# A two-layer decoder trunk on one core: which engine splits the first weights of a stage, and where GpSimd's work stands at the mixers' ends

## The chip, the cores and the metric

The kernel runs on one core of a Trainium2 chip. The core has a matrix engine (TensorE, PE in the profile), three engines for elementwise work (VectorE or DVE, ScalarE or ACT, GpSimd or POOL) and a queue that issues transfers (SyncE or SP). Each runs its own list of instructions in order and waits for others at semaphores. The metric is device time in microseconds; the median of three runs before the change is 2029.25 us.

## The reference, cut to what matters

Two layers on x of 512 tokens by 1024 features, in float32. Each layer is feed-forward, token mixer, feed-forward, and each of these stands between two RMS norms:

```
hf = swiglu(rms_norm(x, g[0]), gate, up, down);  x = x + 0.5 * rms_norm(hf, g[1])
xn = rms_norm(x, g[2]);  mix = attention(xn) or mlstm(xn);  x = x + rms_norm(mix, g[3])
hf = swiglu(rms_norm(x, g[4]), gate, up, down);  x = x + 0.5 * rms_norm(hf, g[5])
swiglu(x) = (silu(x @ gate) * (x @ up)) @ down          # inner width 2816 = 22 x 128
```

Layer 0 mixes with attention (eight stick-breaking heads, eight dilated heads), layer 1 with an mLSTM. So there are six stages, called f00, att, f01, f10, mls and f11 in the code.

## The kernel before, in words

Every float32 factor of a product is split in two: a high part, rounded by a cast on ScalarE (whi, xnh, hhi, dhi), and the rest, found by a subtraction (wlo, xnl, hlo, dlo). A product is then three TensorE instructions: high by high, high by low, low by high (`mm3`). A weight chunk of 128 by 1024 is loaded by SP into one of three buffers called raw, cast to whi on ScalarE, and subtracted to wlo (`chunk`). A raw buffer is free for the next load when the subtraction is done, and a whi buffer (four of them inside a stage) when TensorE has used it.

The tokens are in four blocks of 128 (tb 0 to 3). x and the stage's result y are kept with tokens on partitions; xnh and xnl hold the normalized x transposed. TensorE transposes it into PSUM (tiles pt), ScalarE copies the high part and VectorE takes the low part from PSUM. The first products of a stage go over its first weights twice, for tokens 0 to 255 (the first half) and for 256 to 511.

Between two stages stands, for each block, a chain: y gets its last product (po, added by VectorE from PSUM), y times the gain is yg, ScalarE sums the squares, GpSimd takes the inverse root r of a 128x1 column, VectorE updates x; then squares, root and gain again give the input of the transposition. Behind a feed-forward this is `chain` and `pre` (L276 writes xa and xb, L281 transposes), and the first four chunks of the next stage come from `first_chunks`, with the subtraction on GpSimd, pinned in program order. The first of mls is a small gate chunk, always on VectorE. Behind a mixer it is `out_last`, written out by hand: `load`, `hi` and `lo` are the three steps of a chunk (six chunks, numbered 0 to 5), `add`, `sq`, `mul`, `root`, `upd` and `xs` the chain's, `tp` the transposition (L614), `xn` the two parts of xnh and xnl. Operations on VectorE, ScalarE and GpSimd in there are pinned in the written order and have the line number L51 of the helper that pins them.

The order of everything else is set by a planner that walks a clock of TensorE time and wakes waiting tasks; the table W holds delays for it. `l2` and `l3` say how long after the written part the transpositions of blocks 2 and 3 come in TensorE's list.

Of the kernel before, what the change touches and what calls it, by code (L numbers as in the profile page):

```python
# [24 lines left out]
OFF, OFFV = 80, 48  # L25
# [7 lines left out]
STARTE = (0, 3)  # L33
# [4 lines left out]
       "g6", "o2", "g7")  # L38
W = dict(pdf=9000, pda=4000, pdm=4000, lane=14464, sb1=11880, sb2=6132, d1=14281, d2=3450, qs=6662, end=2121, tz=12960, m0=7140, m1=9600, m2=4263,
         cv=12909, og=1942, mend=5400, avs=2127, mvs=3369, ac1=4899, mc1=4987, ac2=3992, mc2=4402, fc1=5500, fc2=4500,  # L40
         pre=3900, l2=12800, l3=15800, x00=6863, x01=5227, x02=1924, x03=0, x10=7176, x11=2670, x12=1796, x13=0)


class Pinned:
# [9 lines left out]
class Trunk:  # L54
# [109 lines left out]
    def first_chunks(self, ph, between=None, pool=None):  # L164

        a, g = self.a, self.nc.gpsimd
        if ph == "att":
            srcs = [(a["attn_in"][c], 1024) for i in ORD[:2] for c in ((i, 4 + i) if i < 4 else (8 + i, 12 + i))]
        elif ph == "mls":
            srcs = [(a["gates"], 0)] + [(a["mlstm_in"][i], 1024) for i in (0, 8, 1)]  # L170
        else:
            l, w = int(ph[1]), int(ph[2])
            srcs = [(a[n][l, w, f], 1024) for f in (0, 1) for n in ("gate", "up")]
        self.cs = []

        def task():
            for i, (s, n) in enumerate(srcs):
                self.cs.append(self.chunk(s, pool=pool, shift=OFF, eng=None if between and i in STARTE else g) if n else
                               self.gates(s))
                if between and i:  # L180
                    between(i + 1) if i < 3 else None
                yield W["x%s%d" % (ph[1], i)] if pool else self.w_pre
        self.spawn(task(), 0 if pool or between else W["pd" + ph[0]])
        self.tick()
# [23 lines left out]
    def gain(self, l, i, pool=None):  # L208
        wide = pool and pool is self.xpool
        g = (pool or self.pp).tile([P, D], F32, tag="gb" if wide else "dr" if pool else "gp", bufs=1,  # L210
                                   name="gb")
        self.nc.sync.dma_start(g, self.a["norm_g"][l * 6 + i:l * 6 + i + 1, :].partition_broadcast(P))
        return g
# [75 lines left out]
    def half(self, h):  # L289

        self.require(lambda: {2 * h, 2 * h + 1} <= self.xn_done)
        if h:
            self.xn_done.clear()
# [252 lines left out]
    def out_last(self, ws, mix, po, done, nxt, gain):  # L546
# [5 lines left out]
        g = gain(None)  # L552
        xp = self.xpool = tc.alloc_tile_pool(name="xp", bufs=1, side="right", reuse_waits="tile")
        V, A, G = [Pinned(tc, e) for e in (nc.vector, nc.scalar, nc.gpsimd)]
# [4 lines left out]
        def load(i):  # L559
            raws[i] = self.pp.tile([P, 1024], F32, tag="raw", bufs=3, name="raw")  # L560
            nc.sync.dma_start(raws[i], srcs[i])

        def hi(i):
            pool = xp if i < 4 else None
            self.cs.append([self.whole(t, t, OFF - 64 if pool else OFF, pool) for t in ("whi", "wlo")])
            A.copy(self.cs[i][0], raws[i])

        def lo(i, e):
            e.tensor_sub(self.cs[i][1], raws[i], self.cs[i][0])
# [4 lines left out]
        def add(tb, h):  # L574
            V.tensor_add(self.y[:, tb, half(h)], self.y[:, tb, half(h)], po[tb][h])

        def square(src, h, ss):
            junk = self.pp.tile([P, 512], mybir.dt.bfloat16, tag="junk", bufs=1, name="junk")
            A.activation(junk, src[:, half(h)], AF.Square, accum_out=ss)

        def sq(tb, h, x=False):
            if x:
                ss = self.sums[:, tb, h:h + 1]
            else:
                ss = vs[tb, h] = self.few(self.pp, 1, "ss", 4)
            square((self.x if x else self.y)[:, tb, :], h, ss)

        def mul(tb, h, e):
            if h == 0:
                ygs[tb] = [xp.tile([P, 512], F32, tag="h", bufs=4, name="yg") for _ in range(2)]  # L590
            e.tensor_mul(ygs[tb][h], self.y[:, tb, half(h)], g[:, half(h)])

        def root(tb, x=False):
            acc = EPS
            for h in range(2):
                v = self.few(self.pp, 1, "v", 4)
                V.tensor_scalar(v, self.sums[:, tb, h:h + 1] if x else vs[tb, h], 1.0 / D, acc,
                                op0=ALU.mult, op1=ALU.add)
                acc = v
            rs[tb] = self.few(self.pp, 1, "r", 4)  # L600
            G.tensor_tensor(rs[tb], v, self.mhalf, op=ALU.pow)

        def upd(tb, h):
            xt = self.x[:, tb, half(h)]
            V.scalar_tensor_tensor(xt, ygs[tb][h], rs[tb], xt, op0=ALU.mult, op1=ALU.add)

        def xs(tb, h):
            V.scalar_tensor_tensor(ygs[tb][h], self.x[:, tb, half(h)], rs[tb], gn[:, half(h)],
                                   op0=ALU.mult, op1=ALU.mult)

        def tp(tb, h):
            pts[tb, h] = pt = self.bank("pt")
            for j in range(4):
                nc.tensor.transpose(pt[:, j * P:(j + 1) * P], ygs[tb][h][:, j * P:(j + 1) * P], self.ident)  # L614
                self.clk += 109

        def xn(tb, h, part):
            dst = [c[:, 4 * h:4 * h + 4, tb * P:(tb + 1) * P] for c in (self.xnh, self.xnl)]
            src = pts[tb, h].rearrange("p (k t) -> p k t", k=4)
            if part:  # L620
                V.tensor_sub(dst[1], src, dst[0])
            else:
                A.copy(dst[0], src)
# [5 lines left out]
            self.out_part(ws, mix, po, tb, ks)  # L629
        hi(0)  # L630
        lo(0, G)
        hi(1)
        load(2)
        load(3)
        add(0, 0); sq(0, 0); add(0, 1); sq(0, 1)
# [2 lines left out]
        mul(0, 1, V)  # L638
        root(0)
        add(1, 1); sq(1, 1)  # L640
        mul(1, 0, G)
        upd(0, 0); sq(0, 0, True); upd(0, 1); sq(0, 1, True)
        mul(1, 1, V)
        root(1)
# [4 lines left out]
        tp(0, 0); tp(0, 1)  # L649
        xn(0, 0, 0); xn(0, 1, 0)  # L650
        xs(1, 0); xs(1, 1)
        tp(1, 0); tp(1, 1)
        xn(0, 0, 1); xn(0, 1, 1)
        xn(1, 0, 0); xn(1, 1, 0)
        hi(2)
        lo(1, G)
        hi(3)
        xn(1, 0, 1); xn(1, 1, 1)
        self.xn_done |= {0, 1}

        load(4)
        lo(3, G)
        add(2, 0); sq(2, 0); add(2, 1); sq(2, 1)
        add(3, 0); sq(3, 0); add(3, 1); sq(3, 1)
        lo(2, V)
        load(5)
        mul(2, 0, G); mul(3, 0, G)
        mul(2, 1, V); mul(3, 1, V)
        root(2)
        hi(4)  # L670
        upd(2, 0); sq(2, 0, True); upd(2, 1); sq(2, 1, True)
        root(3)
        lo(4, V)
        upd(3, 0); sq(3, 0, True); upd(3, 1); sq(3, 1, True)
        hi(5)
        root(2, True)
        root(3, True)
        xs(2, 0); xs(2, 1)
        lo(5, V)
        xs(3, 0); xs(3, 1)  # L680

        def late(tb, wait):
# [615 lines left out]
```

## Time and profile before

| what | value |
|---|---|
| runs | 2024.54, 2029.25, 2032.24 us |
| profiled execution | 2027.32 us, of which the span of the trace is 2025.6 us |
| TensorE busy | 1965.8 us, 97% |
| VectorE, ScalarE, GpSimd busy | 1318.1, 954.5, 498.2 us |
| mean granted clock of TensorE | 0.99 of full speed |

TensorE has work nearly all the time, so the time that can be won by moving other engines' work lies in the few places where it waits or runs at half clock. These are the ends of stages. The engines of a row say who worked; in the timeline, the bracket behind a row gives the idle time of the engine before it, and what ended that.

### The profile page before, as it was taken

The page shows a single profiled execution, that of the slowest core. Times are in us where ns is not written, and L with a number is a line of the kernel's source. Part 1 is how long each engine was busy: PE and PEld are TensorE (multiplying, and loading weights), DVE is VectorE, ACT ScalarE, POOL GpSimd, SP SyncE. Part 2 cuts the span into 40 slices and gives each one's busy share as a digit, 9 for nine tenths or more (in the row PEclk, how much of TensorE's full clock was granted, in tenths as well). Part 3 has the DMA queues.
Part 4 walks back from the last instruction along what each step waited for, and adds up shares of the span by engine and source line. Part 5 has one row for each costly group of instructions (what it writes and reads, how often), then busy time and mean ns, then how long its engine had stood idle before and what let it go on. Part 6 is the DMA issues. An engine that isn't in the chain of part 4 may idle for free. (4 is left out here: it accounts for less than half of the span.)

```text
span 2025.6 us, 25972 instructions
## 1 busy us (share of the span) xinstructions
PE 1965.8 (97%) x9876; PEld 1664.9 (82%) x9876; DVE 1318.1 (65%) x2018; ACT 954.5 (47%) x1649; POOL 498.2 (25%) x372
## 2 busy tenths in 40 slices
PE   8999999999999999999999999999999999999998
PEld 7888888888887878888788888888889878888887
DVE  6766654666678775664487666547776787676643
ACT  5443333477786453333244333324887644433321
POOL 4332312101002342221343232121010143332111
PEclk9999999999999999999999999999999999999999
DMA  5423332232221333233123333321423222433321
GB/s 180 132 94 105 104 111 75 81 113 68 68 73 58 108 122 108 96 110 117 54 84 126 104 104 105 115 68 54 154 100 126 92 85 96 132 94 114 105 84 42
DMA packets 56119, 200.51 MB, mean 99 GB/s; under 512 B 6521, under 2 KB 6649, under 8 KB 55994
## 3 DMA queue, kind: packets, MB, share of 16 engines
q1 hardware_dynamic: 55992, 198.85, 29.8%
q8 instruction: 77, 1.26, 0.3%
q14 instruction: 48, 0.39, 0.1%
q10 hardware_dynamic: 2, 0.00, 0.0%
HBM read 196.65 MB, written 4.80 MB: 99 GB/s over the span
## 5 line engine op out<-in xcount | busy, mean ns | idle before, releaser
L83 PE MATMUL pg<-xnh,whi 128*128 128x512 f32 (+1 forms) x1568 | 576.8, 369 | 3.9 <-ACT xnh L51 2.0
L83 PE MATMUL pg<-xnh,wlo 128*128 128x512 f32 (+1 forms) x1568 | 577.1, 368 | 3.4 <-DVE wlo L51 3.4
L83 PE MATMUL pg<-xnl,whi 128*128 128x512 f32 (+1 forms) x1568 | 577.5, 369 | 0.9 <-DVE xnl L205 0.5
L148 ACT CAST whi<-raw 128x1024 fp32r<-128x1024 f32 x236 | 247.5, 1051 | 430.6 <-issue 190.7
L149 DVE TENSOR_TENSOR wlo<-raw,whi 128x1024 fp32r<-128x1024 f32 x223 | 284.9, 1279 | 185.9 <-ACT whi L148 181.8
L83 PEld LDWEIGHTS pg<-xnh,wlo 128*128 128x128 f32 x1568 | 297.0, 189 | 53.5 <-DVE wlo L51 4.2
L83 PEld LDWEIGHTS pg<-xnh,whi 128*128 128x128 f32 x1568 | 296.4, 190 | 54.1 <-ACT xnh L51 2.9
L83 PEld LDWEIGHTS pg<-xnl,whi 128*128 128x128 f32 x1568 | 297.3, 190 | 50.3 <-DVE xnl L51 1.0
L414 POOL TENSOR_TENSOR h<-h,rs 128x512 f32<-128x512 f32 x88 | 143.1, 1626 | 755.7 <-ACT h L413 755.7
L205 DVE TENSOR_TENSOR dlo<-raw,dhi 128x512 fp32r<-128x512 f32 x240 | 189.4, 809 | 88.9 <-ACT dhi L204 88.5
L204 ACT CAST dhi<-raw 128x512 fp32r<-128x512 f32 x240 | 146.6, 622 | 195.8 <-DMA raw<-down 152.1
L415 DVE TENSOR_TENSOR h<-h,pg 128x512 f32<-128x512 f32 x88 | 60.0, 682 | 205.7 <-PE pg L83 197.2
L83 PE MATMUL pc<-dhi,hhi 128*128 128x512 f32 x448 | 175.2, 391 | 5.1 <-ACT hhi L204 5.1
L83 PE MATMUL pc<-dhi,hlo 128*128 128x512 f32 x448 | 175.1, 391 | 0.3 <-DVE hlo L205 0.3
L83 PE MATMUL pc<-dlo,hhi 128*128 128x512 f32 x448 | 174.9, 390 | 0.0
L499 DVE TENSOR_TENSOR y<-y,pc 128x512 f32<-128x512 f32 x192 | 128.6, 677 | 5.5 <-PE pc L83 5.4
L83 PE MATMUL pq<-xnh,whi 128*128 128x512 f32 (+1 forms) x312 | 109.9, 353 | 0.8 <-DVE ql L791 0.8
L83 PE MATMUL pq<-xnl,whi 128*128 128x512 f32 (+1 forms) x312 | 109.7, 352 | 0.3 <-DVE xnl L205 0.3
L83 PE MATMUL pq<-xnh,wlo 128*128 128x512 f32 (+1 forms) x312 | 109.2, 350 | 0.0
L205 DVE TENSOR_TENSOR hlo<-h,hhi 128x256 fp32r<-128x256 f32 x208 | 103.1, 514 | 8.1 <-ACT hhi L204 7.9
L204 ACT CAST hhi<-h 128x256 fp32r<-128x256 f32 x208 | 78.9, 404 | 55.2 <-DVE h L415 48.3
L83 PEld LDWEIGHTS pc<-dhi,hhi 128*128 128x128 f32 x448 | 84.4, 188 | 23.3 <-ACT hhi L204 6.0
(257 smaller groups left out, 3318.4 us busy)
## 6 DMA issues: line engine op xcount, KB each, us to landing
raw<-gate SPq DMA_DIRECT2D x88, 512.0 KB, 3.4
raw<-up SPq DMA_DIRECT2D x88, 512.0 KB, 3.4
raw<-down SPq DMA_DIRECT2D x88, 512.0 KB, 3.5
raw<-mlstm_in SPq DMA_DIRECT2D x24, 512.0 KB, 3.5
raw<-attn_in SPq DMA_DIRECT2D x16, 512.0 KB, 3.4
bt<-rows SPq DMA_DIRECT2D x8, 896.0 KB, 4.2
gb<-norm_g SPq DMA_DIRECT2D x11, 512.0 KB, 3.6
raw<-attn_v SPq DMA_DIRECT2D x8, 512.0 KB, 9.0
```

Source lines behind the costliest of these rows:

```text
L83: self.nc.tensor.matmul(out, lhsT=lhsT, rhs=rhs, start=start, stop=stop, skip_group_check=True)
L148: nc.scalar.copy(hi[:, :n], raw[:, :n])
L149: sub = (eng or nc.vector).tensor_sub(lo[:, :n], raw[:, :n], hi[:, :n])
L204: self.nc.scalar.copy(hi, src)
L205: self.nc.vector.tensor_sub(lo, src, hi)
L414: self.nc.gpsimd.tensor_mul(h, h, self.rs)
L415: self.nc.vector.tensor_mul(h, h, pu)
L499: self.nc.vector.tensor_add(dst, dst, b)
```

## The change

Three things change. Behind a feed-forward, the first chunks of the next stage are subtracted on VectorE, where the planner may place them, and no longer on GpSimd. At a mixer's end, GpSimd gives three of its four products of y with the gain to VectorE and keeps the roots and three subtractions (chunks 0, 1 and 2; before 0, 1 and 3), and the casts and subtractions stand at other places. And block 2's transposition is planned later (`l2`, `l3`).

```
-  pre=3900, l2=12800, l3=15800, ...
+  pre=3900, l2=15000, l3=16500, ...
 first_chunks:
-  self.chunk(s, pool=pool, shift=OFF, eng=None if between and i in STARTE else g) if n else ...
+  self.chunk(s, pool=pool, shift=OFF, eng=g if between and i not in STARTE else None) if n else ...
 out_last:
         hi(0)
         lo(0, G)
-        hi(1)
...
-        mul(1, 0, G)
+        mul(1, 0, V)
...
         xs(1, 0); xs(1, 1)
+        hi(1)
+        lo(1, G)
         tp(1, 0); tp(1, 1)
...
         hi(2)
-        lo(1, G)
-        hi(3)
+        lo(2, G)
...
+        add(2, 0); sq(2, 0); add(2, 1); sq(2, 1)
+        hi(3)
+        add(3, 0); sq(3, 0); add(3, 1); sq(3, 1)
         load(4)
-        lo(3, G)
...
-        lo(2, V)
         load(5)
-        mul(2, 0, G); mul(3, 0, G)
-        mul(2, 1, V); mul(3, 1, V)
+        lo(3, V)
         root(2)
+        mul(2, 0, V); mul(2, 1, V)
         hi(4)
         upd(2, 0); sq(2, 0, True); upd(2, 1); sq(2, 1, True)
         root(3)
         lo(4, V)
+        mul(3, 0, V); mul(3, 1, V)
+        hi(5)
         upd(3, 0); sq(3, 0, True); upd(3, 1); sq(3, 1, True)
-        hi(5)
         root(2, True)
+        lo(5, V)
         root(3, True)
         xs(2, 0); xs(2, 1)
-        lo(5, V)
         xs(3, 0); xs(3, 1)
```

On VectorE the four subtractions (wlo) now stand in the list of the old stage, beside the last gated products h and their splits hlo; this is the end of f00, and f01 reads alike.

```order
 L205 TENSOR_TENSOR hlo<-h,hhi 128x256 x2
 L205 TENSOR_TENSOR dlo<-raw,dhi 128x512 x2
-L415 TENSOR_TENSOR h<-h,pg 128x512
+L149 TENSOR_TENSOR wlo<-raw,whi 128x1024
+L415 TENSOR_TENSOR h<-h,pg 128x512
+L149 TENSOR_TENSOR wlo<-raw,whi 128x1024
 L205 TENSOR_TENSOR hlo<-h,hhi 128x256 x2
-L415 TENSOR_TENSOR h<-h,pg 128x512
+L149 TENSOR_TENSOR wlo<-raw,whi 128x1024
+L415 TENSOR_TENSOR h<-h,pg 128x512
```

So the subtractions have left the stretch of the chains and stand before the last split of h.

GpSimd's list at a mixer's end, before:

```order
L51 TENSOR_TENSOR wlo<-raw,whi 128x1024
L51 TENSOR_TENSOR yg<-y,gb 128x512
L51 TENSOR_TENSOR r<-v,mhalf 128x1
L51 TENSOR_TENSOR yg<-y,gb 128x512
L51 TENSOR_TENSOR r<-v,mhalf 128x1 x3
L51 TENSOR_TENSOR wlo<-raw,whi 128x1024 x2
L51 TENSOR_TENSOR yg<-y,gb 128x512 x2
L51 TENSOR_TENSOR r<-v,mhalf 128x1 x4
```

and after, up to the first product of the feed-forward:

```order
L51 TENSOR_TENSOR wlo<-raw,whi 128x1024
L51 TENSOR_TENSOR yg<-y,gb 128x512
L51 TENSOR_TENSOR r<-v,mhalf 128x1 x4
L51 TENSOR_TENSOR wlo<-raw,whi 128x1024 x2
L51 TENSOR_TENSOR r<-v,mhalf 128x1 x4
L414 TENSOR_TENSOR h<-h,rs 128x512 x2
```

Three products with the gain are gone, one between the first two roots and two before the last four.

ScalarE's list at the end of att, before, from the cast of chunk 4 (raw_5890) on; raw_6431 and raw_6462 are chunks 6 and 7, which the feed-forward itself loads:

```order
L51 CAST whi_5926<-raw_5890 128x1024
L51 ACTIVATE junk_5930,sums_75<-x_71 128x512
L51 ACTIVATE junk_5933,sums_75<-x_71 128x512
L51 ACTIVATE junk_5943,sums_75<-x_71 128x512
L51 ACTIVATE junk_5946,sums_75<-x_71 128x512
L51 CAST whi_5948<-raw_5910 128x1024
L51 CAST xnh_73<-pt_6102 128x4x128
L51 CAST xnh_73<-pt_6107 128x4x128
L148 CAST whi_6433<-raw_6431 128x1024
L51 CAST xnh_73<-pt_6137 128x4x128
L51 CAST xnh_73<-pt_6142 128x4x128
```

and after, where chunk 4 is raw_5907:

```order
L51 CAST whi_5922<-raw_5907 128x1024
L51 ACTIVATE junk_5926,sums_75<-x_71 128x512
L51 ACTIVATE junk_5929,sums_75<-x_71 128x512
L51 CAST whi_5942<-raw_5909 128x1024
L51 ACTIVATE junk_5946,sums_75<-x_71 128x512
L51 ACTIVATE junk_5949,sums_75<-x_71 128x512
L148 CAST whi_6433<-raw_6431 128x1024
L51 CAST xnh_73<-pt_6123 128x4x128
L51 CAST xnh_73<-pt_6128 128x4x128
L51 CAST xnh_73<-pt_6137 128x4x128
L51 CAST xnh_73<-pt_6142 128x4x128
```

The cast of chunk 6 stood between the copies of block 2 and block 3 and now stands before all four.

## Rows read from the trace of the kernel before

**Rows 1.** Windows: length, busy time (instructions) of PE, PEld, DVE, ACT, POOL, then clock.
```profile
640.00:680.00 40.00, 31.76 (x217) 28.80 (x216) 33.42 (x59) 17.78 (x37) 14.29 (x11) 0.91 0.27 90
685.00:690.00 5.00, 5.00 (x46) 5.00 (x46) 1.82 (x4) 1.42 (x3) 1.72 (x2) 1.00 0.47 189
975.00:1000.00 25.00, 25.00 (x112) 20.67 (x112) 9.94 (x14) 6.63 (x15) 7.45 (x6) 1.00 0.07 22
1000.00:1040.00 40.00, 35.23 (x214) 30.79 (x213) 32.53 (x54) 12.92 (x33) 15.60 (x14) 0.91 0.20 66
1014.00:1021.00 7.00, 5.91 (x19) 4.61 (x18) 5.27 (x10) 1.99 (x6) 1.83 (x2) 0.51 0.23 75
```

**Rows 2.** Waits of PE, f00 to att (335 to 372): total, times, longest.
```profile
PE pt L281 <- DVE xb L276: 1.2, 1, 1.2
PE po L83 <- ACT hhi L204: 1.1, 1, 1.1
PE pt L281 <- DVE xa L276: 0.6, 2, 0.4
```

**Rows 3.** Waits of PE, f01 to f10 (985 to 1030).
```profile
PE pt L281 <- DVE xa L276: 2.5, 1, 2.5
PE pt L281 <- DVE xb L276: 1.8, 2, 1.1
```

**Rows 4.** Timeline of DVE and POOL, end of f01: start, length, what.
```profile
992.78 2.40 POOL L149 TENSOR_TENSOR wlo<-raw,whi 128x1024 fp32r<-128x1024 f32 x1
992.85 3.54 DVE L306 SCALAR_TENSOR_TENSOR x<-yg,r,x 128x512 f32<-128x512 f32 x2 [0.66 <-POOL r L239]
...
1028.85 1.41 DVE L306 SCALAR_TENSOR_TENSOR x<-yg,r,x 128x512 f32<-128x512 f32 x2 [0.73 <-POOL r L239]
```

**Rows 5.** Timeline of DVE and POOL, end of att, blocks 0 and 1.
```profile
633.79 2.41 POOL L51 TENSOR_TENSOR wlo<-raw,whi 128x1024 fp32r<-128x1024 f32 x1 [48.10 <-PE po L83]
634.06 1.88 DVE L51 TENSOR_TENSOR y<-y,po 128x512 f32<-128x512 f32 x3 [0.59 <-PE po L83]
...
638.39 1.29 POOL L51 TENSOR_TENSOR yg<-y,gb 128x512 f32<-128x512 f32 x1
638.46 2.43 DVE L51 SCALAR_TENSOR_TENSOR x<-yg,r,x 128x512 f32<-128x512 f32 x2 [0.72 <-POOL r L51]
...
646.26 2.34 POOL L51 TENSOR_TENSOR wlo<-raw,whi 128x1024 fp32r<-128x1024 f32 x1
646.33 3.48 DVE L51 SCALAR_TENSOR_TENSOR yg<-x,r,gb 128x512 f32<-128x512 f32 x2 [0.66 <-POOL r L51]
```

**Rows 6.** Timeline of PE, ends of att and (from 1649) of mls.
```profile
644.67 1.32 PE L614 MATMUL pt<-ident,yg 128*128 128x128 f32 x8 [0.64 <-DVE yg L51]
649.20 1.97 PE L614 MATMUL pt<-ident,yg 128*128 128x128 f32 x8 [3.21 <-DVE yg L51]
...
651.72 0.58 PE L83 MATMUL pg<-xnl,whi 128*128 128x256 f32 x1
...
678.01 0.39 PE L83 MATMUL pg<-xnl,whi 128*128 128x256 f32 x1 [0.40 <-DVE xnl L51]
...
1649.91 1.31 PE L614 MATMUL pt<-ident,yg 128*128 128x128 f32 x8 [0.42 <-DVE yg L51]
...
1682.69 0.31 PE L83 MATMUL pg<-xnl,whi 128*128 128x256 f32 x1
```

**Rows 7.** Timeline, end of att: a root, and chunk 6.
```profile
663.47 1.22 DVE L51 TENSOR_TENSOR wlo<-raw,whi 128x1024 fp32r<-128x1024 f32 x1
663.70 1.39 POOL L51 TENSOR_TENSOR r<-v,mhalf 128x1 f32<-128x1 f32 x1 [1.98 <-DVE v L51]
...
670.23 0.33 SPq L146 DMA_DIRECT2D raw<-gate  x1
...
675.06 1.04 ACT L148 CAST whi<-raw 128x1024 fp32r<-128x1024 f32 x1 [2.86 <-DMA raw<-gate]
```

**Rows 8.** Page, part 6: issues, size, median us to landing.
```profile
raw<-gate SPq DMA_DIRECT2D x88, 512.0 KB, 3.4
```

More of the change, by code (lines that the diff above doesn't have):

```diff
@@ L40 @@
          cv=12909, og=1942, mend=5400, avs=2127, mvs=3369, ac1=4899, mc1=4987, ac2=3992, mc2=4402, fc1=5500, fc2=4500,
-         pre=3900, l2=12800, l3=15800, x00=6863, x01=5227, x02=1924, x03=0, x10=7176, x11=2670, x12=1796, x13=0)
+         pre=3900, l2=15000, l3=16500, x00=6863, x01=5227, x02=1924, x03=0, x10=7176, x11=2670, x12=1796, x13=0)
 class Pinned:
@@ L177, in task @@
             for i, (s, n) in enumerate(srcs):
-                self.cs.append(self.chunk(s, pool=pool, shift=OFF, eng=None if between and i in STARTE else g) if n else
-                               self.gates(s))
+                self.cs.append(self.chunk(s, pool=pool, shift=OFF, eng=g if between and i not in STARTE else None)
+                               if n else self.gates(s))
                 if between and i:
@@ L655, in out_last @@
         hi(2)
-        lo(1, G)
-        hi(3)
+        lo(2, G)
         xn(1, 0, 1); xn(1, 1, 1)
         self.xn_done |= {0, 1}
+        add(2, 0); sq(2, 0); add(2, 1); sq(2, 1)
+        hi(3)
+        add(3, 0); sq(3, 0); add(3, 1); sq(3, 1)
         load(4)
-        lo(3, G)
-        add(2, 0); sq(2, 0); add(2, 1); sq(2, 1)
-        add(3, 0); sq(3, 0); add(3, 1); sq(3, 1)
-        lo(2, V)
         load(5)
-        mul(2, 0, G); mul(3, 0, G)
-        mul(2, 1, V); mul(3, 1, V)
+        lo(3, V)
         root(2)
+        mul(2, 0, V); mul(2, 1, V)
         hi(4)
```

## The prediction

> **What bounds the kernel now.** I read the page first: TensorE is busy 97% of the span, so only the stretches where it is not busy, or runs slowly, can give anything. Then the windows view, first over the whole span and then over the ends of stages. The reader is to see that steady stretches show TensorE busy without a break (975 to 1000: 25.00 of 25), while 640 to 680 (end of att) and 1000 to 1040 (end of f01) show 31.76 and 35.23 of 40, with a mean clock of 0.91 [rows 1]. The clock's mean hides its two levels: from 1014 to 1021 it is 0.51, which is the lower level of 1.2 GHz for the whole stretch, right behind a wait [rows 1]. Then the waits of TensorE at these ends: it waits for the transpositions' inputs xa, xb and yg from VectorE [rows 2, 3, 6]. Last, the timeline of VectorE and GpSimd there, which says why the inputs are late. Two updates of x take 1.41 us when GpSimd is idle, and 3.54 us when a 2.40 us subtraction of GpSimd starts 0.07 us before them: they lose 2.1 us, nearly the whole subtraction [rows 4]. The same happens at the mixer's end: 3.48 us for the pair that TensorE waits 3.21 us for [rows 5, 6]. But three additions that read po from PSUM take 1.88 us, 0.63 each, beside a GpSimd subtraction [rows 5]: they lose nothing. So what bounds the ends of stages is VectorE, held up by GpSimd where it takes two operands from SBUF.
>
> **End of f01 (part one of the change).** Four subtractions leave GpSimd. Their durations on VectorE are 1.22 us each [rows 7], 4.9 us in all, and by the order they now stand in the tail of the feed-forward, where VectorE is busy 9.94 of 25 us [rows 1]; that idle time hides them. If the cover were gone, each end would lose what stands ahead of the last hlo, one subtraction of 1.2 us, so 3.7 us at three ends. What goes: TensorE's waits of 2.5 and 1.8 us [rows 3], since block 0 gets its 2.1 us back at the first update, and block 1 again, and VectorE then arrives before TensorE. The half clock that follows the wait goes too: 5.91 us of work between 1014 and 1021 at 0.51 would take half, so 2.9 us come back [rows 1]. Sum: 4.3 + 2.9 = 7.2 us. What is late next: the chains of blocks 2 and 3, whose additions wait for TensorE itself, so they move forward with it.
>
> **End of f00 and of f10.** The same waits, smaller: 1.2 + 0.6 us at both (the second shows the same two rows), no half clock. At f00 there is 1.1 us more: the last hhi stands on ScalarE behind the cast of the fourth chunk, whose load waits for a raw buffer that GpSimd frees late [rows 2]. With the first subtraction done in the tail the load is early. Sum: 2.9 and 1.8 us.
>
> **Ends of att and mls (part two).** I follow one chain, from TensorE's arrival A (644.03 in att: 644.67 less the 0.64 it waited [rows 6]).
> Block 0: the updates of x take 1.41 instead of 2.43 us, as the product on GpSimd beside them is gone [rows 5]; the product on VectorE that replaces it falls into the wait for the root. So xs of block 0 is 1.0 us earlier and the wait of 0.64 goes.
> Block 1: its pair starts 1.0 us earlier and takes 1.41 instead of 3.48, so it ends at A + 2.7 instead of A + 5.8, and the transpositions end at A + 3.4. The subtraction that was beside the pair (chunk 1) now waits for a cast behind block 0's copies and runs beside the four xnl, which read PSUM, so I cost it at nothing; if it came early it would cost 2.1 us again.
> Four xnl at 0.63 each follow, and the first product that needs the third starts at S = A + 4.6, where it started at A + 7.7 (651.72 [rows 6]). Gain so far 3.1 us.
> From S, VectorE's list: the last xnl 0.6, four additions 2.5, a subtraction 1.2 (and 0.8 until its cast is there), four small columns 0.7, two pairs of products and two of updates at 1.41, and two subtractions at 1.2, in all 13.9 us to the end of chunk 5.
> The roots stay on GpSimd and now start beside VectorE's products: before, one that began beside a VectorE subtraction took 1.39 us and ended 0.4 us after it [rows 7]. Two of the four are on the path, so 0.9 us: S + 14.8.
> On this place the Trainium skill (SBUF — State Buffer, section "Who interferes with whom") speaks against the change: it says that the pair of ports which VectorE and GpSimd share is locked for a whole instruction by whichever starts first, so products moved to VectorE can hold up the roots as the subtractions held up VectorE. By it alone each of four roots could lose a whole product of 0.7 us, 2.8 us per mixer's end; by the row it is 0.4 us each.
> Chunk 5's buffer then takes chunk 6. Its cast now stands on ScalarE before all four copies of blocks 2 and 3. In att the load took 4.83 us from issue to cast (670.23 to 675.06 [rows 7]); as the other bound I take 3.4, the median to landing of such loads [rows 8]. So the cast starts at S + 18.2 to 19.6. It takes 1.04, then VectorE's subtraction 1.2 and three xnl 1.9: the second half runs freely from S + 22.3 to 23.8, which is A + 26.9 to 28.4.
> TensorE's own work is not the limit: 144 products at 5/46 = 0.11 us [rows 1] and the transpositions end at about S + 18.5. So a new wait of 4 to 5 us stands here.
> Before, the same point was at 678.01, A + 34.0. Gain 5.6 to 7.1, taken as 6.2 us. In mls it was 1682.69, from 1649.49, so A + 33.2 [rows 6]; the same steps give 4.8 to 6.3, and I take 5.0, since the first root is ready earlier there and hides less of the product that moves to VectorE.
>
> **The sum.** 2.9 + 6.2 + 7.2 + 1.8 + 5.0 = 23.1 us. The new wait of 4 to 5 us is longer than the one of 2.5 us that half clock followed, and I charge one such stretch of 2.9 us for the two mixer's ends. That leaves 20.2 us. The profiled execution took 2027.32 us (1.7 us outside its span), so it would take 2007; it lay 1.9 us under the median of 2029.25, so the median goes to 2009.
>
> **The rivals.**
> 1. The mixers' ends give nothing. Chunk 6's cast is the place: it stands before all four copies, and each microsecond of its load is one of TensorE's wait. For: TensorE already waited at this point (0.40 us for xnl at 678.01 [rows 6]) with one block's copies behind that cast, and now two blocks' stand behind it. Against: even a load of 4.83 us leaves 5.6 us of gain. It decides when load, queue and a half-clock stretch together cost 6 us more than I count. Then 11.9 us remain: 2017, between 2012 and 2021.
> The Trainium skill (TensorE: Matmul & The Clock Gate, section "Part 1: The HAM clock gate") would help this rival: it says that the throttled clock is the default, released by activity and back after idling. The trace agrees at 1014, where 0.51 follows a wait of 2.5 us; by it both new waits would cost 2.9 us, and the gain would be 17.3 us.
> 2. Behind the feed-forwards another wait takes over. VectorE's list is in order, and block 2's addition stands behind block 1's last steps. For: block 2 came just in time before, and it is the next thing TensorE needs. Against: VectorE is relieved of 2.1 us for each collision and its additions wait for TensorE. If it takes half of these 11.9 us back, 14 us of gain stay, 2015; if all, 8 us, 2021.
> 3. Slower: VectorE becomes the bound. It decides if the long updates are not GpSimd's doing, so that they stay long, and VectorE's idle time in the tails is not to be had because the casts come late. VectorE then has 11 subtractions of 1.22 and six products of 0.71 more, 17.7 us, on the path: 2047. For: it is the second busiest engine, 33.42 of 40 us at the mixer's end [rows 1]. Against: the long pairs are long by nearly the length of the GpSimd instruction beside them, three times in the rows [rows 4, 5].
>
> **How the numbers follow.** My forecast has 0.64, with its own range of 2004 (nothing charged for the clock, and both upper ends of the mixers' gains: 25.3 us) to 2013 (the lower ends, and two stretches of half clock). Rival 1 has 0.16, rival 2 has 0.13, rival 3 has 0.07. About 0.5%, 10 us, is what a measurement of this kernel can tell from no change, so faster means below 2019. Of rival 1 a quarter, of rival 2 a half, and of rival 3 a third lies within: same is 0.04 + 0.07 + 0.02 = 0.13, slower 0.05, faster 0.82. The range of 2000 to 2021 takes in the forecast, most of rivals 1 and 2, and below 2004 what TensorE may save in later waits that I left alone.
>
> **What would show it.** In the changed profile: no wait of TensorE for xa or xb at the end of f01, and clock 1.00 there; pairs of updates at 1.41 us everywhere; the subtractions of chunk 1 and 2 beside xnl and y, which stay at 0.63 each; TensorE waiting 4 to 5 us for xnh before the second half, with the cast of chunk 6 as the one that waits for its load; roots of 1.0 to 1.4 us. It is wrong if VectorE's pairs stay near 3.5 us, if wlo is what the last products of a feed-forward wait for, or if half clock is found in as many stretches as before.

## The result and the profile after

The changed kernel takes 1999.8 us (median of four runs, 1998.43 to 2002.11) where the kernel before took 2028.97 us beside it: a ratio of 0.9859, with a 95% interval of 0.9838 to 0.988. So it is faster by 29 us; 20 were forecast (2009 us, between 2004 and 2013). The profiled execution took 1998.43 us with a span of 1996.7 us.

The first part of the page, with the busy time of each engine:

```profile
PE 1958.3 (98%) x9876; PEld 1662.1 (83%) x9876; DVE 1300.9 (65%) x2035; ACT 955.8 (48%) x1649; POOL 463.6 (23%) x355
```

TensorE has 7.5 us less busy time for the same 9876 instructions, for the most part because it ran less at the lower clock (some 5 us, see the paragraph on the clock); the other 21 us of the span were waits. VectorE, which took over subtractions and products, is busy 17 us less: what it no longer spends being held up by GpSimd is more than what it took over.

Windows of the trace after (length, busy time of PE, PEld, DVE, ACT, POOL, then granted clock, share of the DMA engines and GB/s): the end of att, TensorE's second half there, the tail of f01, the end of f01, the second half behind mls, and the start of f11.

```profile
627.00:667.00 40.00, 37.17 (x253) 33.34 (x253) 34.57 (x70) 23.95 (x49) 15.19 (x12) 0.96 0.34 106
658.00:664.00 6.00, 4.72 (x39) 4.06 (x38) 5.08 (x14) 3.30 (x5) 0.00 (x0) 1.00 0.30 100
955.00:980.00 25.00, 25.00 (x112) 20.72 (x111) 9.60 (x16) 6.37 (x12) 4.09 (x4) 1.00 0.26 85
980.00:1020.00 40.00, 40.00 (x256) 36.00 (x255) 29.55 (x59) 15.43 (x39) 10.49 (x13) 1.00 0.08 27
1644.00:1651.00 7.00, 4.24 (x28) 3.57 (x27) 5.75 (x15) 3.42 (x6) 0.00 (x0) 0.87 0.28 87
1690.00:1697.00 7.00, 6.42 (x15) 4.72 (x16) 5.45 (x12) 4.00 (x9) 0.95 (x1) 0.51 0.60 212
```

The end of f01 is without a gap: 40.00 of 40 at full clock, where [rows 1] had 35.23 of 40 at 0.91. The four subtractions did go into the tail's idle time: three of them lie in the row 955 to 980, where VectorE is busy 9.60 of 25 us with them, and TensorE waits for none. The last row shows a stretch at 1.2 GHz that before did not have at this place.

The end of f01 on VectorE and GpSimd, beside [rows 4]:

```profile
979.29 1.41 DVE L306 SCALAR_TENSOR_TENSOR x<-yg,r,x 128x512 f32<-128x512 f32 x2 [0.66 <-POOL r L239]
982.52 1.85 DVE L276 SCALAR_TENSOR_TENSOR xa<-x,r,gb 128x512 f32<-128x512 f32 x1
982.53 1.29 POOL L300 TENSOR_TENSOR yg<-y,gb 128x512 f32<-128x512 f32 x1
```

The pair of updates takes 1.41 us, not 3.54. One collision is left (xa takes 1.85 beside GpSimd's yg), but TensorE waits for neither xa nor xb there.

The end of att after, on TensorE, VectorE, GpSimd, ScalarE and SP's queue, beside [rows 5 to 7]:

```profile
637.22 1.21 PE L614 MATMUL pt<-ident,yg 128*128 128x128 f32 x8
639.58 1.32 PE L614 MATMUL pt<-ident,yg 128*128 128x128 f32 x8 [1.15 <-DVE yg L51]
642.03 0.44 PE L83 MATMUL pg<-xnl,whi 128*128 128x256 f32 x1 [0.21 <-DVE xnl L51]
659.86 1.04 PE L614 MATMUL pt<-ident,yg 128*128 128x128 f32 x8
662.10 1.25 PE L614 MATMUL pt<-ident,yg 128*128 128x128 f32 x8 [1.20 <-DVE xnl L51]
664.22 0.32 PE L83 MATMUL pg<-xnl,whi 128*128 128x256 f32 x1
```

```profile
638.77 1.42 DVE L51 SCALAR_TENSOR_TENSOR yg<-x,r,gb 128x512 f32<-128x512 f32 x2 [0.66 <-POOL r L51]
640.10 2.48 DVE L51 TENSOR_TENSOR xnl<-pt,xnh 128x512 fp32r<-128x512 f32 x4
642.49 2.47 DVE L51 TENSOR_TENSOR y<-y,po 128x512 f32<-128x512 f32 x4
648.38 1.41 DVE L51 SCALAR_TENSOR_TENSOR x<-yg,r,x 128x512 f32<-128x512 f32 x2
652.42 1.41 DVE L51 SCALAR_TENSOR_TENSOR x<-yg,r,x 128x512 f32<-128x512 f32 x2
654.13 1.22 DVE L51 TENSOR_TENSOR wlo<-raw,whi 128x1024 fp32r<-128x1024 f32 x1
661.36 1.28 DVE L51 TENSOR_TENSOR xnl<-pt,xnh 128x512 fp32r<-128x512 f32 x2
```

```profile
640.08 4.86 POOL L51 TENSOR_TENSOR wlo<-raw,whi 128x1024 fp32r<-128x1024 f32 x2 [1.35 <-ACT whi L51]
647.40 0.86 POOL L51 TENSOR_TENSOR r<-v,mhalf 128x1 f32<-128x1 f32 x1 [2.46 <-DVE v L51]
650.31 1.39 POOL L51 TENSOR_TENSOR r<-v,mhalf 128x1 f32<-128x1 f32 x1 [2.05 <-DVE v L51]
```

```profile
655.37 0.33 SPq L146 DMA_DIRECT2D raw<-gate  x1
659.13 1.05 ACT L148 CAST whi<-raw 128x1024 fp32r<-128x1024 f32 x1 [4.39 <-DMA raw<-gate]
660.50 1.07 ACT L51 CAST xnh<-pt 128x512 fp32r<-128x512 f32 x2 [0.31 <-PE pt L614]
```

GpSimd's two subtractions (4.86 us) run beside eight operations of VectorE that read one operand from PSUM, and these take 0.62 us each: nothing is lost. The wait for block 1's transposition fell from 3.21 to 1.15 us, that for block 0 is gone. Before the second half TensorE waits 1.20 us, and not for xnh: the transposition of block 3 waits for VectorE's read of block 2's pt (xnl, from 661.36). The kernel has eight tiles in PSUM (banks, `bufs=8`); six hold pg of the first chunks, and block 2's two pt have the others until xnl has read them.

### The profile page after: what moved, and what is told of

Same layout as the page of the kernel before. It is cut to its first block, busy times and chain, and to the rows that moved or that the text cites. A ratio compares the mean times of both kernels' runs of the same rounds, so it can differ in the third digit from the quotient of the medians.

```text
span 1996.7 us, 25967 instructions
## 1 busy us (share of the span) xinstructions
PE 1958.3 (98%) x9876; PEld 1662.1 (83%) x9876; DVE 1300.9 (65%) x2035; ACT 955.8 (48%) x1649; POOL 463.6 (23%) x355
## 4 chain that ended last, share of the span: by engine, by line
PE 83%; DVE 6%; ACT 6%; issue 2%; POOL 2%; DMA 1%; SPq 0%; POOLq 0%; DVEq 0%; ACTq 0%
PE pg L83 45%; PE pc L83 15%; PE po L83 9%; PE pq L83 6%; PE pv L83 4%; PE ob L83 2%; PE z L83 1%; ACT p5hi L204 1%; DVE dlo L205 1%; DVE yg L51 1%; PE pt L281 1%; DVE wlo L149 1%; ACT whi L148 1%; DVE p5lo L205 1%; ACT e L876 0%
## 5 line engine op out<-in xcount | busy, mean ns | idle before, releaser
L149 DVE TENSOR_TENSOR wlo<-raw,whi 128x1024 fp32r<-128x1024 f32 x234 | 298.6, 1278 | 197.8 <-ACT whi L148 191.8
```

What stands on the lines that cost most here:

```text
L149: sub = (eng or nc.vector).tensor_sub(lo[:, :n], raw[:, :n], hi[:, :n])
```

## The experiments

To place the gain I compare when the same TensorE instruction starts in two traces. The difference between before and the changed kernel, and what it grows by at each place, in one profiled execution of each (us):

| place | forecast | after | part one alone (e1) | part two alone (e2) |
|---|---|---|---|---|
| end of f00 | 2.9 | 6.0 | 6.0 | 0 |
| end of att | 6.2 | 6.9 | 0.1 | 3.1 |
| end of f01 | 7.2 | 7.9 | 7.9 | 0.3 |
| end of f10 | 1.8 | 4.9 | 4.9 | 0.3 |
| end of mls | 5.0 | 5.3 | 0.7 | 6.4 |
| start of f11 | 0 | -2.6 | -1.7 | -1.6 |

The column of after adds up to 28.4 us; 0.7 more stand in the kernel's first 100 us, where nothing was changed. The 2.9 us that the forecast took off for half clock at the mixers' ends are not in its column.

**e1 and e2: each part alone.**

```diff
 e1, on before, first_chunks:
-eng=None if between and i in STARTE else g
+eng=g if between and i not in STARTE else None
 e2: after, with this line put back
```

> Before, with part one alone: the first chunks behind a feed-forward are split on VectorE; the mixers' ends and the plan are as before. Theory: each part pays where it stands, and what the trace after showed at the ends of f00, f01 and f10 (5.7 + 8.1 + 4.6 us of TensorE's list moved forward) belongs to this part alone: 18.4 us, so 2010 to 2011 us. Rival: only the terms of the prediction (2.9 + 7.2 + 1.8 = 11.9 us) belong to it, and the 6 us above them came from the mixers' ends upstream (another clock, other buffers): 2017 us.

> After, with the first chunks behind a feed-forward back on GpSimd: part two alone (mixers' ends and plan). Theory: the trace after gained 6.7 us at the end of att and 5.2 at the end of mls, and lost 2.2 to half clock in f11 behind the wait for hhi: 9.7 to 12 us, so 2017 to 2019 us. Rival: the mixers' ends gain little alone, and the sum of both parts is more than each by itself: 2023 us or more.

e1: 2009.16 us, ratio 0.9906 (0.989 to 0.9921), 19.3 us faster. e2: 2017.88 us, ratio 0.995 (0.9937 to 0.9962), 10.6 us faster. The sum is 29.9, the change gave 29.2: the totals add up, and each part pays at its own places. Place by place the sum holds behind the feed-forwards; at the end of att the parts give 3.2 us where both together gave 6.9, and at mls 7.1 for 5.3. So the 7 us more than forecast at the feed-forwards' ends (18.8 for 11.9) belong to part one. At the end of att e2 gained only 3.1 us: TensorE and the chunk 6 that its second half hangs on, on SP's queue, ScalarE and TensorE:

```profile
661.74 0.33 SPq L146 DMA_DIRECT2D raw<-gate  x1
667.74 1.04 ACT L148 CAST whi<-raw 128x1024 fp32r<-128x1024 f32 x1 [6.63 <-DMA raw<-gate]
670.69 1.25 PE L614 MATMUL pt<-ident,yg 128*128 128x128 f32 x8 [3.65 <-DVE xnl L51]
```

This load took 6.0 us from issue to cast, where it took 3.8 after; the wait grew from 1.20 to 3.65 us with it, and half clock follows it (0.60 from 672 to 676).

**e3: GpSimd kept busy, the work elsewhere unchanged.**

```diff
 after, first_chunks, behind each chunk:
+w = self.cs[-1]
+keep_in_program_order(g.tensor_sub(self.spare, w[1], w[0]))
```

> After, with a useless subtraction of 128x1024 on GpSimd (wlo less whi into a spare tile that nobody reads) at each place in its list where before had the split of a first chunk. VectorE, ScalarE, TensorE and the queue have the lists of after; no buffer waits for the useless work. Theory (GpSimd beside VectorE): VectorE's two-operand updates are held up as before, pairs of 1.41 us go back to 3.5, and the 18.4 us of the feed-forwards' ends are lost but for the 1 to 2 us that an earlier cast of the fourth chunk gave at the end of f00: 2016 to 2018 us. Rival (buffers): the gain came from raw buffers freed earlier and from casts and loads that moved into the tail, and GpSimd's work beside does nothing: 2000 us.

2013.27 us, ratio 0.9925 (0.9911 to 0.9938). The end of f01 on GpSimd, VectorE and TensorE, and the end of f00 on TensorE:

```profile
983.00 2.39 POOL L183 TENSOR_TENSOR spare<-wlo,whi 128x1024 fp32r<-128x1024 f32 x1
983.07 3.54 DVE L310 SCALAR_TENSOR_TENSOR x<-yg,r,x 128x512 f32<-128x512 f32 x2 [0.66 <-POOL r L243]
1003.70 0.66 PE L285 MATMUL pt<-ident,xa 128*128 128x128 f32 x4 [2.47 <-DVE xa L280]
```

```profile
365.16 0.66 PE L285 MATMUL pt<-ident,xa 128*128 128x128 f32 x4 [0.39 <-DVE xa L280]
367.02 0.66 PE L285 MATMUL pt<-ident,xb 128*128 128x128 f32 x4 [1.20 <-DVE xb L280]
373.77 0.39 PE L84 MATMUL pq<-xnl,whi 128*128 128x256 f32 x1 [0.34 <-DVE xnl L209]
377.16 0.63 PE L285 MATMUL pt<-ident,xa 128*128 128x128 f32 x4 [0.83 <-DVE xa L280]
```

Work that nobody waits for brings back the pair of 3.54 us and the wait of 2.5 [rows 3, 4], and at the end of f00 every wait of [rows 2] but that for hhi, which the early cast had removed. Of the gains at the ends of f00, f01 and f10 it takes 4.3 of 6.0, 7.4 of 7.9 and 4.6 of 4.9 us. So VectorE was held up by GpSimd's neighbourhood; what is left for buffers and earlier casts is some 1.7 us, at f00. The total lost only 13.5 us of these 16.3, since two stretches at half clock that after has, in the middle of att (410 to 414) and half of that in f11, were not there in this run.

**e4: one subtraction back beside two-operand work, at the mixers.**

```diff
 after, out_last:
         lo(0, G)
+        hi(1)
...
         root(1, True)
+        lo(1, G)
...
         xs(1, 0); xs(1, 1)
-        hi(1)
-        lo(1, G)
```

> After, with one thing moved at the two mixers' ends: the cast of chunk 1 is early, as in before, so GpSimd's split of it runs beside the second scaling pair of VectorE (block 1's input of the transposition) and not beside the reads of PSUM behind it. The amount of work is that of after. Theory: that pair takes 3.5 us for 1.42, TensorE waits 2.1 us longer for block 1's transposition at both mixers, and half clock follows that wait as it did before (up to 1.7 us more at each): 2004 to 2008 us. Rival (the place of a split does not matter, the mixers' gain is that GpSimd has fewer products and the four copies come later): 2000 us, pair at 1.4.

2001.98 us, ratio 0.9873 (0.9853 to 0.9893): the interval overlaps that of after, so the total settles nothing. The trace does, here on GpSimd, VectorE and TensorE:

```profile
640.19 2.34 POOL L51 TENSOR_TENSOR wlo<-raw,whi 128x1024 fp32r<-128x1024 f32 x1
640.26 3.48 DVE L51 SCALAR_TENSOR_TENSOR yg<-x,r,gb 128x512 f32<-128x512 f32 x2 [0.66 <-POOL r L51]
643.13 1.77 PE L614 MATMUL pt<-ident,yg 128*128 128x128 f32 x8 [3.21 <-DVE yg L51]
```

The pair takes 3.48 us and TensorE waits 3.21, as before [rows 5, 6]. The gain at the end of att falls from 6.9 to 3.4 us and that at mls from 5.3 to 4.7, but f11 loses 0.1 and not 2.6, because its wait of 2.55 us for hhi was not followed by half clock in this run.

**e5: the planned delays of before.**

```diff
-l2=15000, l3=16500
+l2=12800, l3=15800
```

> After, with the two planned delays of before: block 2's transposition comes 2.2 us of TensorE's work earlier, which also puts block 2's copies ahead of the cast of chunk 6 on ScalarE. Theory (the second half waits for the PSUM banks that block 2's low parts free, and these stand behind that cast): the wait of 2.7 us for xnl at the end of mls shrinks by 1 us or more, and the half clock behind it may go; 1996 to 1999 us. Rival (the later plan is what the mixers' gain needs, because an early transposition makes TensorE wait for VectorE's scaling): 2001 to 2004 us.

1995.46 us, ratio 0.9832 (0.9819 to 0.9846); its four runs lie at 1992.98 to 1996.6, all below those of after, though the two intervals overlap at their ends (0.9838 to 0.9846). By starts it gives 1.4 us at the end of att and 3.0 at mls. So this piece of the change costs about 4 us. The end of mls on TensorE (block 2's transposition, then block 3's) and on ScalarE:

```profile
1641.42 1.32 PE L614 MATMUL pt<-ident,yg 128*128 128x128 f32 x8 [0.57 <-DVE yg L51]
1645.06 1.03 PE L614 MATMUL pt<-ident,yg 128*128 128x128 f32 x8
```

```profile
1642.12 1.25 ACT L51 CAST xnh<-pt 128x512 fp32r<-128x512 f32 x2 [2.55 <-PE pt L614]
1643.55 1.05 ACT L148 CAST whi<-raw 128x1024 fp32r<-128x1024 f32 x1 [0.18 <-DMA raw<-gate]
```

Block 2's copies now stand ahead of chunk 6's cast, the banks are free in time, and block 3's transposition waits for nothing; in after it waited 2.70 us at this place:

```profile
1648.04 1.27 PE L614 MATMUL pt<-ident,yg 128*128 128x128 f32 x8 [2.70 <-DVE xnl L51]
```

**e6: the three products back on GpSimd.**

```diff
-mul(1, 0, V) ... mul(2, 0, V) ... mul(3, 0, V)
+mul(1, 0, G) ... mul(2, 0, G) ... mul(3, 0, G)
```

> After, with the three products with the gain back on GpSimd at their places in the written order; the subtractions stay where they are. Theory (GpSimd beside VectorE's two SBUF operands): the first update pair takes 2.4 us for 1.41, and the products of blocks 2 and 3 hold up updates too; 1 to 3 us at each mixer's end, 2002 to 2006 us. Rival (the work counts, not the neighbour): VectorE is relieved of three products, 2.0 us at each mixer's end, 1996 to 1998 us.

2005.16 us, ratio 0.9882 (0.9869 to 0.9896), 5.4 us slower than after: the intervals overlap at their ends, but its fastest run, 2004.84, lies above the slowest of after, 2002.11. VectorE's updates of blocks 0 and 2 at the end of att:

```profile
634.07 2.44 DVE L51 SCALAR_TENSOR_TENSOR x<-yg,r,x 128x512 f32<-128x512 f32 x2 [0.37 <-POOL r L51]
652.74 1.42 DVE L51 SCALAR_TENSOR_TENSOR x<-yg,r,x 128x512 f32<-128x512 f32 x2 [1.70 <-POOL yg L51]
```

The first pair is held up (2.44), the second waits 1.70 us for GpSimd's slower product. The three products cost less on the busier engine.

**e7: chunk 6 earlier.**

```diff
         lo(4, V)
+        hi(5)
+        lo(5, V)
         mul(3, 0, V); mul(3, 1, V)
-        hi(5)
...
-        lo(5, V)
```

> After, with the cast and the subtraction of chunk 5 ahead of block 3's products, so that chunk 6's load starts 2.5 us earlier at each mixer's end. Theory (the chain through chunk 6 holds block 2's copies in mls): the wait of 2.7 us there falls to under 1 and its half clock goes; in att, where block 2's copies wait for TensorE itself, 0.3 us at most: 1996 to 1998 us. Rival (the wait ends with block 3's own scaling, which now comes 1.2 us later): 2000 to 2002 us.

1996.85 us, ratio 0.9843 (0.983 to 0.9856): 3 us faster by the medians, but the interval overlaps that of after. The wait before block 3's transposition in mls is 2.07 us for 2.70, in att 0.96 for 1.20: it moves the way the theory says, by less (under 1 was expected in mls). By starts the edit gives 0.2 us in att and 0.6 in mls. The largest difference from after in this profile, 2.6 us at the start of f11, is not the edit's: half clock did not follow the wait for hhi there.

**e8: hhi.** Before and after alike, TensorE waits 2.5 us for hhi at the start of f01 and f11. A feed-forward's product with down is taken in groups of seven products of sums and differences (Strassen's scheme), and this hhi is a factor of such a product.

```diff
 ffn, up_to:
-for _ in range(2):
+for _ in range(1 if f == 4 and n == "gate" and len(cs) == 6 else 2):
```

> After, with TensorE's order changed at the start of f01 and f11 alone: the second product of the first Strassen group comes one projection (about 5.4 us) later. Theory: the wait of 2.5 us for hhi there, which stands in before and after alike, goes, and with it the half clock behind it (3.4 us of it in f01 and 6.8 in f11, half of which is lost): 2.5 + 1.7 + 2.5 + 3.4 = 10.1 us, 1990 us. Rival (VectorE is late by more than one product's place there): the wait moves to the next product, 1998 to 2000 us.

1993.84 us, ratio 0.9824 (0.981 to 0.9837), 6 us faster than after. Windows at the start of f01 and of f11:

```profile
695.00:715.00 20.00, 19.18 (x84) 15.26 (x83) 16.75 (x23) 11.62 (x21) 7.97 (x5) 1.00 0.50 159
1680.00:1700.00 20.00, 19.17 (x84) 15.23 (x83) 16.75 (x23) 11.47 (x21) 8.05 (x5) 1.00 0.52 157
```

Both are at full clock and hold 84 instructions; in after the windows of 20 us around the same waits hold 70 at 0.91 (695 to 715) and 64 at 0.83 (1682 to 1702). A wait of 0.8 us for a later copy is left at each. By the comparison of starts the edit gives 3.2 us at f01 and 4.5 at f11 against after, 7.7 of the 10.1 expected; 2.2 us are lost at the end of att, where chunk 6's load took 5.9 us in this profile, with a wait of 3.29 us behind it.

**e9 and e10: together.** e9 has the edits of e5 and e8, e10 that of e7 too.

> After, with the planned delays of before and with the second product of the first Strassen group one projection later. Theory (each takes away a wait of its own: the banks at the mixers' ends, hhi behind them): 4.3 + 6.0 us add up, 1989 to 1990 us. Rival (both shorten the same stretch, since a wait that goes brings TensorE earlier to the next one): 1992 to 1994 us.

> The same, with the cast and subtraction of chunk 5 early as well. By the order of ScalarE the cast of chunk 6 then stands ahead of block 2's copies again, with its load 2.5 us earlier. Theory (the load, not the place of the cast, is what the copies wait for): 1988 us. Rival (the place of the cast counts): 1992 to 1994 us.

e9: 1988.44 us, ratio 0.9801 (0.9787 to 0.9815). e10: 1988.29 us, ratio 0.9805 (0.9792 to 0.9819). The two edits add up (4.3 + 6.0 were to give 1989.5); the third adds nothing to them. Nor does the cast of chunk 6, ahead of block 2's copies again, cost anything with its load early, as the theory of e10 had it (1988). e9 beats both kernels, by 11 and by 40 us.

**e11: no product on GpSimd behind a feed-forward.**

```diff
 chain:
-nc.gpsimd.tensor_mul(yg[0], yt[:, :512], g[:, :512])
+nc.vector.tensor_mul(yg[0], yt[:, :512], g[:, :512])
```

> After, with the first half of y times the gain behind a feed-forward on VectorE too, so that GpSimd has nothing but roots there. It takes away the last two-operand work of GpSimd in that stretch (1.29 us, beside which xa takes 1.85 for 0.74 us). Theory (a collision costs only where TensorE waits for its result, and at the ends of f00, f01 and f10 TensorE waits for nothing any more): no change, 1999 to 2001 us, perhaps 2 us more if VectorE's 0.7 us a block come on the path of the last chain. Rival (every collision counts): three to four pairs a stage become 1.1 us shorter, 1990 us or less.

1999.17 us, ratio 0.9858 (0.9843 to 0.9873): no change, and by starts none above 0.1 us at the ends of f00, f01 and f10. In VectorE's timeline xa is fast, and still nothing is gained:

```profile
987.12 0.75 DVE L276 SCALAR_TENSOR_TENSOR xa<-x,r,gb 128x512 f32<-128x512 f32 x1
```

## Why the prediction was right, and where it was not

The direction and the mechanism were right, the size was not: 29 us for 20.2. The median of 1999.8 us lies under the forecast's own range of 2004 to 2013 and at the lower edge of 2000 to 2021.

**Ends of the feed-forwards.** The mechanism was right in each point: pairs at 1.41, no wait for xa or xb, clock 1.00. Two terms were mis-sized, those of f00 (2.9 forecast, 6.0 measured) and f10 (1.8 and 4.9), for two reasons. First, I summed the waits of [rows 2], whose window ends at 372, and let the waits of the blocks behind it stand; e3 shows that those of 0.34 and 0.83 us are the same collisions, handed down VectorE's list. "What is late next" was answered rightly (blocks 2 and 3 move forward with TensorE), but by that answer their waits had to go too. Second, the wait in a row of TensorE is less than what the step costs. Before, the weight loader's rows at this place:

```profile
367.87 0.42 PEld L281 LDWEIGHTS pt<-ident,xa 128*128 128x128 f32 x4 [0.79 <-DVE xa L276]
369.73 0.42 PEld L281 LDWEIGHTS pt<-ident,xb 128*128 128x128 f32 x4 [1.44 <-DVE xb L276]
```

and TensorE's after:

```profile
364.56 0.60 PE L281 MATMUL pt<-ident,xa 128*128 128x128 f32 x4
365.00 0.60 PE L281 MATMUL pt<-ident,xb 128*128 128x128 f32 x4
```

From xa's start to xb's it was 1.86 us and is 0.44: 1.42 gained, where TensorE's row had said 1.2 [rows 2] and the loader's says 1.44. Over the six waits at f00 the first reason is worth 1.2 us and the second some 2; at f10 they are worth 1.6 and 1.5. At f01 the three waits gave 4.9 us for 4.3, a wait for xnl that was not in the sum 0.6, and the clock 2.4 for 2.9.

What a collision costs VectorE is not what it costs TensorE. At f00 before, block 0's pair of updates stood beside two subtractions:

```profile
349.26 5.21 POOL L149 TENSOR_TENSOR wlo<-raw,whi 128x1024 fp32r<-128x1024 f32 x2
349.32 5.69 DVE L306 SCALAR_TENSOR_TENSOR x<-yg,r,x 128x512 f32<-128x512 f32 x2 [0.66 <-POOL r L239]
```

It lost 4.3 us, and TensorE waited 0.2 us for that block's xa.

**Ends of the mixers.** The sizes were nearly right (6.2 and 5.0 forecast, 6.9 and 5.3 measured). Measured on the chain in att: S is A + 4.8 (4.6 forecast), chunk 5's split ends at S + 13.3 (14.8), chunk 6's cast starts at S + 17.1 (18.2 to 19.6), the second half runs freely from A + 27.0 (26.9 to 28.4). In mls it does so from A + 27.7 (1650.82, from 1623.16). That the end of the chain came out is in part luck, since two errors cancel: the cast came 1.1 to 2.5 us early, and from it to the free run it took 5.1 us where 4.1 were counted. The failed step is "a new wait of 4 to 5 us" for xnh. TensorE waits 1.20 us in att and 2.70 in mls, and for a bank, one transposition earlier: block 3's, which cannot start before block 2's low parts are out. I had looked for the data that the second half needs and not for the place that its transposition writes to; and I had not priced the changed plan, by which both transpositions stand behind all of the first half. e5 prices it at 4 us against the change.

The roots took 0.86 us beside a product and 1.39 beside a subtraction, for 0.55 alone, and ended 0.4 us after the instruction that they had met, as [rows 7] had it: beside a product 0.3 us were lost, not the whole 0.7. The 0.9 us charged for them on the path did not come: VectorE's updates at 648.38 and 652.42 wait for no root. By the Trainium skill (SBUF — State Buffer, section "Who interferes with whom"), a VectorE instruction with at most one SBUF input, outside the modes in which it uses both ports, stays clear of GpSimd, and one with two contends with a GpSimd instruction that reads SBUF; here 0.62 us for reads of PSUM, and 3.54 for 1.41 with two SBUF operands, agree with it.

**The clock.** One stretch of half clock, 2.9 us, was charged to the mixers' ends. One did follow the new wait of 2.70 us in mls (0.57 from 1649 to 1653); it costs some 1.7 us, an estimate from half of the time at 1.2 GHz there, and is part of the 5.3. None followed that of 1.20 us in att. That the total has the 2.9 us all the same is luck: 2.6 us were lost at the start of f11, where a wait of 2.55 us for hhi that stood there before, too, was now followed by 0.51 from 1690 to 1697. Over windows of 1 us from 300 to 1760, time at the lower clock fell from about 34 to 24 us, so some 5 of the 28.9 us of the span are the clock's. The prediction named as a sign of being wrong that half clock is found in as many stretches as before: there it is found in six, where before had seven.

**The rivals.** Chunk 6's cast (rival 1) does hold the mixers' second half, in mls and with a slow load; in att block 2's copies waited another 0.31 us for TensorE's own transposition. But its worst load here, 6.0 us in e2, cost 3.8 us of the gain at that end (2.5 in the wait, the rest at half clock), never the 6 that the rival needs. Nothing took over behind the feed-forwards (rival 2): their ends gave more than forecast. VectorE as the bound (rival 3) is out: 29.55 of 40 us busy at the end of f01, with TensorE at 40.00.

## What to carry to other kernels

Where GpSimd and VectorE work side by side, place GpSimd's long two-operand work beside VectorE's reads of PSUM, or give it to VectorE in a stretch where that idles: each collision cost nearly the whole GpSimd instruction, but only where TensorE waited for the result (e3 against e11). When a delay is removed from an in-order list, every later wait that it was handed down to goes with it, and starts of the same instruction in two traces size this better than the sum of listed waits. When a step is moved, look also for the buffer or PSUM bank that it writes to.

## What was not expected of the hardware

The load of the same 512 KB at the end of att took 3.8 us (after), 5.9 (e8) and 6.0 (e2) from issue to cast, and TensorE's wait there grew by the difference, from 1.20 to 3.29 and 3.65 us. What makes the load longer is not shown.

How long a wait is does not say whether half clock follows it. In e8 the wait of 1.14 us at 638.56 is followed by it, that of 3.29 us at 663.18 is not; the windows behind them:

```profile
640.00:646.00 6.00, 5.64 (x31) 5.25 (x32) 5.24 (x9) 5.13 (x12) 3.83 (x2) 0.72 0.38 119
660.00:670.00 10.00, 6.74 (x54) 6.33 (x55) 4.94 (x6) 6.59 (x9) 0.43 (x1) 1.00 0.23 61
```

What decides it stays open here. Stretches of half clock that come and go (f11 in after, e4 and e7) are one reason why single places moved by 1 to 3 us between traces where no edit was; totals a few us apart, as those of after and e4, could not be told apart.
